# The causal convolution's spectra at 128 odd frequencies of 256 points, its wrapped end in one product, and two weight splits moved behind them

## The chip, the cores and the metric

The kernel runs on one core of a Trainium2 chip. The metric is the device time of one execution in microseconds. A core has an engine for matrix products (PE in the profile, its weight loads PEld), three engines for elementwise work (DVE, ACT, POOL) and SP, which here only issues transfers. The engines run their own instruction streams in order and wait for each other through semaphores.

## The reference

One decoder layer for 256 tokens of width 1024, all in float32: a norm, one input projection, then side by side an attention over 8 heads and a convolution module of 512 channels, an output projection with residual, and a SwiGLU network with residual. The part that matters here is the convolution and what surrounds it:

```
h = rms_norm(x, norm1_g)
proj = h @ w_in                        # q, k, v (512 each), u (1024)
a, g = split(u + glu_b)
h = a * sigmoid(g)                     # 256 tokens x 512 channels
h = causal_depthwise_conv(h, dw_w)     # 31 taps in the token direction
h = layer_norm(h + dw_b, ln_g, ln_b)   # over the 512 channels
conv = silu(h)
x = x + concat([attn, conv]) @ w_out
```

## The kernel before

Precision: the kernel writes most factors as a sum of a rounded high part and a low rest (names ending in `h` and `l`), and one product becomes three matmuls (`mm3`: high by high, high by low, low by high). Weights come from memory in blocks of 1 MB (`raw`), each of which is two pieces of 1024 columns. For a piece, ACT writes the high part `wh` and DVE the low part `wl`. `feed(n)` brings the pieces up to number `n` to their end; it is called ahead of the products, so that pieces are a few units ahead of PE. A block's buffer is free when the low part of its second piece has been written; then SP issues the load of the next block.

The order on every engine is that of the program text, and nothing reorders it later. Work beside the products is written as generator tasks; `step()` is called between groups of products and lets every task that is due write its next instructions.

The projections are five chunks of eight units (`p`, 40 units, pieces 0 to 19): k, q, the gate, the convolution's input, v. Tasks then compute the attention (`S`, `sm`, `p`, `pT`) while later chunks are still being multiplied. The output projection (`po`) uses pieces 20 to 27, and the network after it the rest.

The convolution is done with spectra. `spectra_task` turns the 31 taps into spectra `Ws` (one matmul, `pw`, for each of three column groups of the table `taps`). `conv_task` computes the gated input, splits it into `hh` and `hl`, and multiplies it by the table `fwd`: `hf` 0 and 1 are real and imaginary parts at 128 frequencies, `hf` 2 (in `third`, behind the v chunk) has the 17 frequencies that are left over from a transform of 288 points, 68 rows. DVE multiplies the spectra (`ya`, `yb`, `Y`), ACT and DVE split the products (`yh`, `yl`), and `ln_task` transforms back with the table `inv` into `cv` 0 and 1 (128 tokens each; three products of three matmuls for each), on which the channel norm stands (`st`, `mv`, `lr`, `nb`, `yn`). The bias `dw_b` is one row more in `Y` 2, against a row of ones in `inv`. `yn` is turned by PE into `cT`, in the middle of the first half of `po`.

Between `hf` 2 and `cv` PE computes the attention's output `O`: eight heads with two matmuls each in float32, with two heads in the two column halves of the array. `vs` is v scaled by ACT, in two halves for the two token blocks.

Of the kernel before, what the change touches and what calls it, by code (L numbers as in the profile page):

```python
# [9 lines left out]
F32R = mybir.dt.float32r  # L10
# [15 lines left out]
NF = FF // P  # L26
TAPS = 31
EPS = 1e-6
L = 288
NB = 47  # L30
BW = 2048
PIECE = 1024
R3 = 69
WARM = 18
RAW = 4
WGT = 7
# [14 lines left out]
GLU0_WAIT = 3  # L51
L1 = 8
L2 = 28
L3 = 34
W_FIRST = 1
SWAP = 31
SS_WAIT = 4
# [78 lines left out]
def _parts(a):  # L136

    hi = _round12(a)
    return np.stack([hi, a - hi], 1)


def _constants():
    t = np.arange(T)[:, None]
    f = np.arange(L // 2 + 1)[None, :]
    ang = 2 * np.pi * ((t * f) % L) / L
    c, s = np.cos(ang), np.sin(ang)
    alpha = np.where((f == 0) | (f == L // 2), 1.0, 2.0) / L
    fwd = np.concatenate([c[:, :P], -s[:, :P], c[:, P:], -s[:, P:], c[:, P:], -s[:, P:]], 1)
    fwd = _parts(fwd.astype(np.float32).reshape(NT, P, 324).transpose(1, 0, 2))
    ir, ii = (alpha * c).T, (-alpha * s).T  # L150
    inv = np.zeros((3, P, T))
    inv[0], inv[1] = ir[:P], ii[:P]
    inv[2, :R3] = np.concatenate([ir[P:], -ir[P:], ii[P:], ii[P:], np.ones((1, T))], 0)
    inv = _parts(inv.astype(np.float32).transpose(1, 0, 2))
    lag = (TAPS - 1 - np.arange(TAPS))[:, None]
    ang = 2 * np.pi * ((lag * f) % L) / L
    c, s = np.cos(ang), np.sin(ang)
    fw = np.concatenate([c[:, :P], -s[:, :P], c[:, P:], -s[:, P:], -s[:, P:], c[:, P:]], 1)
    fw = fw.astype(np.float32)
    hi = _round12(fw)  # L160
    taps = np.zeros((96, 324), np.float32)
    taps[0:TAPS], taps[32:32 + TAPS], taps[64:64 + TAPS] = hi, hi, fw - hi
    out = {"fwd": fwd, "inv": inv, "taps": taps}
    freq = np.power(np.float32(10000.0), -np.arange(0, HD, 2, dtype=np.float32) / np.float32(HD)).astype(np.float32)
    ang = np.arange(T, dtype=np.float32)[:, None] * freq[None, :]
    cos, sin = np.cos(ang.astype(np.float64)), np.sin(ang.astype(np.float64))
    tab = np.concatenate([cos, cos, -sin, sin], 1).astype(np.float32)
    out["rope"] = np.ascontiguousarray(tab.reshape(NT, P, 2 * HD).transpose(1, 0, 2))
    q, k = np.arange(P)[:, None], np.arange(P)[None, :]
    tri = np.where(k <= q, 0.0, -1e30)  # L170
    out["mask"] = np.concatenate([tri, np.zeros((P, P)), tri], 1).astype(np.float32)
    out["ident"] = np.eye(P, dtype=np.float32)
    return out
# [20 lines left out]
def _build(nc, tc, t, ctx):  # L194
# [12 lines left out]
    def t_bank(name, tag="t"):  # L207
        return psum.tile([P, 512], F32, name=name, tag=tag, bufs=2)
# [176 lines left out]
            load_next()  # L385
    ident = put(const, "ident", [P, P])
    load_next()
    taps = put(early, "taps", [96, 324], tag="Y", bufs=3)
    dwr = early.tile([96, W], F32, name="dwr", tag="Y", bufs=3)
    nc.sync.dma_start(dwr, t["dw_w"])  # L390
    mask = put(early, "mask", [P, 3 * P])
# [32 lines left out]
        G["cols"] = put(const, "cols", [P, 16])  # L424

    def spectra_task():
        tapr = early.tile([96, 324], F32R, name="tapr")
        nc.scalar.activation(tapr, taps, AF.Copy)
        dws = early.tile([96, W], F32R, name="dws")
        nc.scalar.activation(dws, dwr, AF.Copy)  # L430
        nc.vector.tensor_tensor(dws[32:64, :], dwr[32:64, :], dws[32:64, :].bitcast(F32), op=ALU.subtract)
        yield PW_GAP
        Ws = G["Ws"] = early.tile([P, 3, W], F32, name="Ws")
        for j, (o, n) in enumerate(spans):
            b = t_bank(f"pw{j}")
            nc.tensor.matmul(b[:n, :], tapr[:, o:o + n], dws, start=True, stop=True)
            nc.scalar.activation(Ws[:n, j, :], b[:n, :], AF.Copy)
            yield 1
# [50 lines left out]
    def q_task(banks):  # L489
        kqT = keep.tile([P, 2, 4, T], F32, name="kqT", tag="x2T")  # L490
        G["kT"], G["qT"] = kqT[:, 0], kqT[:, 1]
        qr, totals = [], []
        for i in range(NT):
            t1, total = rope_half(banks[i], 0, i, "q")
            totals.append(total)
            qr.append(t1)
            if i == 0:
                yield Q_GAP
        spawn(transposed(qr, G["qT"], "q"), QT_WAIT)
        yield 1  # L500
        for i in range(NT):
            r3 = heads3(G["kr"][i])
            nc.vector.tensor_tensor(r3, r3, cqk[1][:, i, :, None].to_broadcast([P, H, HD]), op=ALU.mult)
        spawn(transposed(G["kr"], G["kT"], "k"), KT_WAIT)
        yield 1
        for total in totals:
            total()
        mean_square(0)
        root(late_part)
        G["scq"] = early.tile([P, NT, H], F32, name="scq")  # L510
        nc.gpsimd.tensor_scalar(G["scq"], cqk[0], HD ** -0.5, None, op0=ALU.mult)
        for name, shape in (("fwd", [P, 2, NT, 324]), ("inv", [P, 2, 3, T])):
            tl = early.tile(shape, F32R, name=name)
            nc.gpsimd.dma_start(tl, t[name])
            G[name] = (tl[:, 0], tl[:, 1])
        yield S_WAIT
        G["sums"] = early.tile([P, NT, H], F32, name="sums")
        G["pT"] = [None] * H
        for j in range(H // 2):
            spawn(pair_task(j), 3 * j)  # L520
# [53 lines left out]
    def conv_task(banks):  # L574
# [3 lines left out]
        for i in range(NT):  # L578
# [6 lines left out]
                nc.vector.tensor_tensor(hl[:, 0, :], us[0], hh[:, 0, :].bitcast(F32), op=ALU.subtract)  # L585
            yield 1
        nc.vector.tensor_tensor(hl[:, 1, :], us[1], hh[:, 1, :].bitcast(F32), op=ALU.subtract)
        yield HF_WAIT
        fwd = G["fwd"]
        hf = []  # L590

        def spectrum(j):
            o, n = spans[j]
            b = t_bank(f"hf{j}", "s" if j < 2 else "t")
            for i in range(NT):
                mm3(b[:n, :], [f[:, i, o:o + n] for f in fwd], (hh[:, i, :], hl[:, i, :]), i == 0, i == NT - 1)
            hf.append(b)
# [12 lines left out]

        def third():

            spectrum(2)
            nc.vector.tensor_tensor(Y[2][:R3 - 1, :], hf[2][:R3 - 1, :], Ws[:R3 - 1, 2, :], op=ALU.mult)

        G["third"] = third
# [8 lines left out]

    def ln_task():
        inv = G["inv"]
        cv = []
        st = early.tile([P, NT, 6], F32, name="st")
        mv = early.tile([P, NT, 2], F32, name="mv")  # L630
        vv = early.tile([P, NT], F32, name="vv")
        for i in range(NT):
            b = t_bank(f"cv{i}", "s")
            for a, j in enumerate(range(3)):
                n = P if j < 2 else R3
                mm3(b, [m[:n, j, i * P:(i + 1) * P] for m in inv], G["ys"][j], a == 0, a == 2)
            cv.append(b)
        yield 1
        for i in range(NT):
            nc.vector.bn_stats(st[:, i, :], cv[i])  # L640
            nc.vector.bn_aggr(mv[:, i, :], st[:, i, :])
        nc.vector.tensor_scalar(vv, mv[:, :, 1], EPS, None, op0=ALU.add)
# [30 lines left out]
    for chunk in range(5):  # L673
        banks = [mm_bank(f"p{chunk}{i}") for i in range(NT)]
        for kt in range(KT):
            step()
            feed(unit // 2 + 1 if unit < L1 else (unit + 3) // 2 if unit < L2 else unit // 2 + (3 if unit < L3 else LEAD))
            w = wtile(unit * W, W)
            unit += 1
            sls = [slice(i * P, (i + 1) * P) for i in range(NT)]  # L680
            order = [(i, a) for i in range(NT) for a in range(3)]
            if W_FIRST < unit <= SWAP:
                order = [(0, 0), (0, 2), (1, 0), (1, 2), (0, 1), (1, 1)]
            for i, a in order:
                nc.tensor.matmul(banks[i], (xh, xh, xl)[a][:, kt, sls[i]], w[a % 2], start=kt == 0 and a == 0,  # L685
                                 stop=kt == KT - 1 and a == 2 - (order[-1][1] == 1))
        if after[chunk]:
            spawn(after[chunk](banks))
# [5 lines left out]
    G["third"]()  # L694
    mix = G["mix"] = [keep.tile([P, KT, T], F32R, name="mix" + s, tag="big_" + s) for s in "hl"]
    O = [None, None]
    for h in range(H):
        feed(unit // 2 + LEAD)
        if h % 2 == 0:
            step()  # L700
        base, pair = (h % 2) * HD, h // 2
        if h % 4 == 0:
            O[h // 4] = mm_bank(f"O{h // 4}").rearrange("p (a q) -> p a q", a=2)
        o = O[pair // 2][base:base + HD, pair % 2, :]
        hs = slice(h * HD, (h + 1) * HD)
        nc.tensor.matmul(o, vs[:, 0, hs], G["pT"][h][:, 0:T], start=True, stop=False)
        nc.tensor.matmul(o[:, P:], vs[:, 1, hs], G["pT"][h][:, T:], start=False, stop=True)
        if h % 4 == 3:
            sl = slice(pair - 1, pair + 1)
            split([m[:, sl, :] for m in mix], O[h // 4], nc.vector)  # L710
    spawn(ln_task())


# [243 lines left out]
def _layout(a):  # L957
# [26 lines left out]
    for n in ("q_norm_g", "k_norm_g"):  # L984
# [7 lines left out]
        "cols": np.concatenate([colize(A["norm2_g"][0]), colize(A["conv_ln_g"][0]), colize(A["conv_ln_b"][0])], 1),  # L992
        "glub": rep(A["glu_b"][0].reshape(2, W)),
        "gqk": rep(np.stack(gqk)),
        "dw_w": np.tile(np.concatenate([A["dw_w"][0], np.zeros((1, W), np.float32)], 0), (3, 1)),
        "dw_b": A["dw_b"],
    }

# [15 lines left out]
```

## Time and profile before

| | |
|---|---|
| runs | 290.14 us median of 3 (289.87 to 290.34) |
| profiled execution | 289.81 us, of which the span from first to last instruction is 288.0 us |
| granted PE clock | 1.00 |
| busy: PE, PEld, DVE, ACT, POOL | 282.5, 229.5, 225.9, 181.3, 24.9 us |
| DMA | 62.84 MB, 218 GB/s over the span |

PE's busy time counts matmuls whose ends are modelled, so 98% does not say that every matmul starts when it could. Start times tell more: consecutive matmuls with 512 columns start about 0.23 us apart, and a larger distance is a wait or a change of kind. In the rows of the timeline the first two columns are the start and the length in us; a number in brackets at a row's end is idle time of that engine before it and what ended it.

### The profile page before, as it was taken

The numbers are of one execution on the slowest core, as the hardware profiler recorded it, in microseconds if no ns is written. First come the engines' busy times: TensorE is split into PE (matmuls) and PEld (weight loads), VectorE is DVE, ScalarE is ACT, GpSimd is POOL, SyncE is SP. The second block draws the span as 40 slices with busy tenths as digits, with TensorE's granted clock in tenths as the row PEclk, the third lists the DMA queues.
The fourth block names the chain that finished last, engine by engine and source line by source line (L and its number), as shares of the span: only waits on it lengthen the run. The fifth ranks groups of instructions, "written<-read, shape, count | busy, mean of one in ns | idle before, by whom it ended". The sixth has DMA issues, their size and how long they took to land.

```text
span 288.0 us, 3690 instructions
## 1 busy us (share of the span) xinstructions
PE 282.5 (98%) x1321; PEld 229.5 (80%) x1321; DVE 225.9 (78%) x339; ACT 181.3 (63%) x271; POOL 24.9 (9%) x46
## 2 busy tenths in 40 slices
PE   8999999999999999999999999999999999999994
PEld 6878877778688888888888888888888888888883
DVE  3899995999973857999997868997787896887211
ACT  5777668989805778654987454795455496656000
POOL 0005473000000000011200011200001020000000
PEclk9999999999999999999999999999999999999999
DMA  7999968743804489368999746699864799400011
GB/s 243 415 413 361 366 218 300 259 152 109 333 1 146 152 316 390 104 216 166 227 352 412 294 150 109 185 229 403 303 259 140 131 239 332 151 1 2 0 73 74
DMA packets 12053, 62.84 MB, mean 218 GB/s; under 512 B 1602, under 2 KB 2210, under 8 KB 6275
## 3 DMA queue, kind: packets, MB, share of 16 engines
q1 hardware_dynamic: 9874, 54.86, 50.3%
q0 software_dynamic: 2016, 7.74, 14.1%
q8 instruction: 10, 0.16, 0.2%
q14 instruction: 9, 0.07, 0.1%
q10 hardware_dynamic: 144, 0.00, 0.0%
HBM read 61.55 MB, written 1.05 MB: 217 GB/s over the span
## 4 chain that ended last, share of the span: by engine, by line
PE 95%; DVE 3%; issue 1%
PE pd L724 21%; PE fg L724 19%; PE p L685 18%; PE U L724 11%; PE po L724 8%; PE V L724 6%; PE W L724 3%; PE aT L805 2%; PE warm L342 1%; PE S L528 1%; PE pT L558 1%; PE x2T L747 1%; PE cv L297 1%; DVE wl L278 0%; PE cv L298 0%
## 5 line engine op out<-in xcount | busy, mean ns | idle before, releaser
L273 ACT ACTIVATE wh<-raw 128x1024 fp32r<-128x1024 f32 x108 | 111.5, 1057 | 40.6 <-DVE raw L272 19.8
L278 DVE TENSOR_TENSOR wl<-raw,wh 128x1024 fp32r<-128x1024 f32 x108 | 129.3, 1221 | 9.3 <-ACT wh L273 8.7
L724 PE MATMUL pd<-wh,act 128*128 128x512 f32 x176 | 57.2, 393 | 0.0
L724 PE MATMUL fg<-wh,g 128*128 128x512 f32 x160 | 52.2, 393 | 0.0
L724 PEld LDWEIGHTS pd<-wh,act 128*128 128x128 f32 x176 | 33.0, 188 | 6.7
L724 PEld LDWEIGHTS fg<-wh,g 128*128 128x128 f32 x160 | 30.0, 188 | 6.1
L724 PE MATMUL pd<-wl,act 128*128 128x512 f32 x88 | 34.3, 389 | 0.0
L685 PE MATMUL p<-wh,xh 128*128 128x512 f32 x80 | 32.9, 412 | 0.0
L685 PE MATMUL p<-wh,xl 128*128 128x512 f32 x80 | 31.3, 392 | 0.0
L724 PE MATMUL fg<-wl,g 128*128 128x512 f32 x80 | 31.1, 389 | 0.0
L685 PE MATMUL p<-wl,xh 128*128 128x512 f32 x80 | 26.7, 395 | 0.0
L286 POOL DMA_DIRECT2D raw<-w x12 | 10.5, 879 | 177.7 <-DVE raw L272 153.3
L724 PEld LDWEIGHTS pd<-wl,act 128*128 128x128 f32 x88 | 16.5, 188 | 3.3
L685 PEld LDWEIGHTS p<-wh,xh 128*128 128x128 f32 x80 | 15.2, 189 | 3.5 <-issue 0.7
L810 DVE TENSOR_TENSOR act<-aT,act 128x512 fp32r<-128x512 f32 (+1 forms) x12 | 7.7, 646 | 12.9 <-ACT act L808 12.9
L685 PEld LDWEIGHTS p<-wl,xh 128*128 128x128 f32 x80 | 15.1, 189 | 3.2 <-DVE wl L278 0.3
L685 PEld LDWEIGHTS p<-wh,xl 128*128 128x128 f32 x80 | 15.1, 189 | 3.1
L724 PEld LDWEIGHTS fg<-wl,g 128*128 128x128 f32 x80 | 15.0, 188 | 3.0
L808 ACT ACTIVATE act<-aT 128x512 fp32r<-128x512 f32 (+1 forms) x12 | 6.6, 560 | 14.8 <-PE aT L805 14.8
L724 PE MATMUL U<-wh,g 128*128 128x512 f32 x48 | 15.8, 390 | 0.0
L272 DVE TENSOR_TENSOR raw<-raw,raw 128x1024 f32<-128x1024 f32 x12 | 14.6, 1218 | 0.0
L724 PE MATMUL po<-wh,mixh 128*128 128x512 f32 x32 | 12.6, 395 | 0.0
(179 smaller groups left out, 413.6 us busy)
## 6 DMA issues: line engine op xcount, KB each, us to landing
raw<-w SPq DMA_DIRECT2D x45, 1024.0 KB, 5.3
raw<-w POOLq DMA_DIRECT2D x12, 512.0 KB, 5.5
first<-first SPq DMA_DIRECT2D x8, 384.0 KB, 6.1
xtok<-xtok SPq DMA_DIRECT2D x2, 512.0 KB, 9.1
x<-xtok SPq DMA_DIRECT2D x2, 512.0 KB, 6.0
out<-o SPq DMA_DIRECT2D x4, 256.0 KB, 2.0
inv<-inv POOLq DMA_DIRECT2D x1, 768.0 KB, 6.9
fwd<-fwd POOLq DMA_DIRECT2D x1, 648.0 KB, 4.0
```

Source lines behind the costliest of these rows:

```text
L272: nc.vector.tensor_tensor(src, src, blocks[add][:, cut(a)], op=ALU.add)
L273: nc.scalar.activation(dst[0], src, AF.Copy)
L278: nc.vector.tensor_tensor(dst[1], src, dst[0].bitcast(F32), op=ALU.subtract)
L286: nc.gpsimd.dma_start(blocks[to][:, cut(a)], t["w"][more - 2][:, cut(a)], accum_op=ALU.add)
L297: nc.tensor.matmul(out, lhs[0], rhs[1], start=False, stop=False)
L342: nc.tensor.matmul(warm[:, 0:T], zeros[:, 0:P], zeros, start=True, stop=True)
L528: nc.tensor.matmul(banks[a][:, out], G["qT"][rows, j, q], G["kT"][rows, j, k], start=True, stop=True)
L685: nc.tensor.matmul(banks[i], (xh, xh, xl)[a][:, kt, sls[i]], w[a % 2], start=kt == 0 and a == 0, stop=kt == KT - 1 and a == 2 - (order[-1] ...
L724: nc.tensor.matmul(bank, l, r, start=start and a == 0, stop=stop and a == 2, skip_group_check=on)
L805: nc.tensor.transpose(b[:, a, :], u[:, a * P:(a + 1) * P], ident)
L808: nc.scalar.activation(hi, b[:, 0:nf, :], AF.Copy)
L810: nc.vector.tensor_tensor(lo, b[:, 0:nf, :], hi.bitcast(F32), op=ALU.subtract)
```

## The change

The transform goes from 288 points to 256 points at the odd multiples of half a step, of which 128 are enough. A product of such spectra is a convolution that wraps with a changed sign: the first 30 outputs get the last taps' share of the last 30 inputs, subtracted. This wrapped end is taken out by a second, small transform of 60 points: the last 32 token rows of `hh`, `hh` and `hl` are copied by three transfers of the POOL queue into three groups of 32 partitions of a new tile `tail`, and `hf` 2 is one matmul of 96 rows against a table `ends` with 120 columns, high and low parts together. Since only the first 30 tokens need it, `cv` 1 (tokens 128 to 255) has no product with `Y` 2; its bias comes from one matmul of the taps' tile `dws` (whose spare rows now hold `dw_b`) with 128 columns more in `tapr`. `cv` 1 is computed ahead of `cv` 0. `Ws`, `Y` and `yl` of index 2 have 120 or 121 rows for 68 or 69; `taps` and `tapr` have 504 columns for 324; `fwd` has 256 columns for 324.

Two things are moved besides. `feed` no longer runs one piece further from unit 34 on, and isn't called between the heads of `O`, so that pieces 23 and 24 get their low parts behind the spectra, and pieces 24 and 25 their high parts. The matmuls of `O` are written with the two heads of a pair in turn.

The core of the diff:

```diff
-L = 288
-R3 = 69
+WRAP = 60
+R3 = 2 * WRAP + 1
+COLS = 2 * P + 2 * WRAP
...
-L3 = 34
...
+    c, s = odd(T, np.arange(T))
+    fwd = _parts(np.concatenate([c, -s], 1).astype(np.float32).reshape(NT, P, T).transpose(1, 0, 2))
...
-    taps = put(early, "taps", [96, 324], tag="Y", bufs=3)
+    taps = put(early, "taps", [96, COLS + P], tag="Y", bufs=3)
...
-        for name, shape in (("fwd", [P, 2, NT, 324]), ("inv", [P, 2, 3, T])):
+        for name, shape in (("fwd", [P, 2, NT, T]), ("ends", [96, R3 - 1]), ("inv", [P, 2, 3, T])):
...
+        tail = early.tile([96, W], F32R, name="tail")
+        for a, part in enumerate((hh, hh, hl)):
+            nc.gpsimd.dma_start(tail[32 * a:32 * a + 32, :], part[96:, 1, :])
         yield HF_WAIT
...
-            spectrum(2)
+            b = t_bank("hf2")
+            hf.append(b)
+            nc.tensor.matmul(b[:R3 - 1, :], G["ends"], tail, start=True, stop=True)
...
-        for i in range(NT):
-            b = t_bank(f"cv{i}", "s")
-            for a, j in enumerate(range(3)):
-                n = P if j < 2 else R3
-                mm3(b, [m[:n, j, i * P:(i + 1) * P] for m in inv], G["ys"][j], a == 0, a == 2)
-            cv.append(b)
+        cv = [t_bank(f"cv{i}", "s") for i in range(NT)]
+        for j in range(2):
+            mm3(cv[1], [m[:, j, P:] for m in inv], G["ys"][j], j == 0, False)
+        nc.tensor.matmul(cv[1], G["tapr"][:, COLS:], G["dws"], start=False, stop=True)
+        for j in range(3):
+            mm3(cv[0], [m[:P if j < 2 else R3, j, :P] for m in inv], G["ys"][j], j == 0, j == 2)
         yield 1
-        for i in range(NT):
+        for i in (1, 0):
             nc.vector.bn_stats(st[:, i, :], cv[i])
...
-            feed(unit // 2 + 1 if unit < L1 else (unit + 3) // 2 if unit < L2 else unit // 2 + (3 if unit < L3 else LEAD))
+            feed(unit // 2 + 1 if unit < L1 else (unit + 3) // 2 if unit < L2 else unit // 2 + 3)
...
-    for h in range(H):
-        feed(unit // 2 + LEAD)
-        if h % 2 == 0:
-            step()
...
+    for pair in range(H // 2):
+        step()
...
+        for i in range(NT):
+            for odd in range(2):
+                h = 2 * pair + odd
+                o = O[pair // 2][odd * HD:(odd + 1) * HD, pair % 2, i * P:]
+                nc.tensor.matmul(o, vs[:, i, h * HD:(h + 1) * HD], G["pT"][h][:, i * T:i * T + T - i * P],
+                                 start=i == 0, stop=i == 1)
```

Where rows move. On DVE, before, between the multiplied spectra and the statistics of the channel norm:

```order
L614 TENSOR_TENSOR Y2_869<-hf2_896,Ws_509 68x512
L278 TENSOR_TENSOR wl24_856<-raw12_616,wh24_855 128x1024
L255 TENSOR_TENSOR yl_911<-Y0_867,yh_910 128x512
L255 TENSOR_TENSOR yl_911<-Y1_868,yh_910 128x512
L255 TENSOR_TENSOR yl_911<-Y2_869,yh_910 69x512
L255 TENSOR_TENSOR mixl_905<-O0_918,mixh_904 128x512
L255 TENSOR_TENSOR mixl_905<-O1_929,mixh_904 128x512
L640 BN_STATS st_944<-cv0_947 128x6
```

The same place of DVE after the change (the names are the same; `wl23` stood ahead of the first `ya` before):

```order
L624 TENSOR_TENSOR Y2_869<-hf2_896,Ws_511 120x512
L260 TENSOR_TENSOR yl_902<-Y0_867,yh_901 128x512
L260 TENSOR_TENSOR yl_902<-Y1_868,yh_901 128x512
L260 TENSOR_TENSOR yl_902<-Y2_869,yh_901 121x512
L260 TENSOR_TENSOR mixl_900<-O0_909,mixh_899 128x512
L260 TENSOR_TENSOR mixl_900<-O1_920,mixh_899 128x512
L283 TENSOR_TENSOR wl23_858<-raw11_583,wh23_857 128x1024
L283 TENSOR_TENSOR wl24_957<-raw12_618,wh24_956 128x1024
L649 BN_STATS st_935<-cv1_939 128x6
```

Two low parts of weights have moved from ahead of `yl` to behind `mixl`, and the statistics stand behind them.

On ACT, before, from the scaled v to the channel norm:

```order
L692 ACTIVATE vs_893<-p40_694,c_179 128x512
L693 ACTIVATE vs_893<-p41_695,c_179 128x512
L273 ACTIVATE wh25_906<-raw12_616 128x1024
L254 ACTIVATE yh_910<-Y0_867 128x512
L254 ACTIVATE yh_910<-Y1_868 128x512
L254 ACTIVATE yh_910<-Y2_869 69x512
L254 ACTIVATE mixh_904<-O0_918 128x512
L254 ACTIVATE mixh_904<-O1_929 128x512
L273 ACTIVATE wh26_1002<-raw13_715 128x1024
L650 ACTIVATE yn0_1020<-cv0_947,nb_992,lr_980 128x512
```

And after:

```order
L701 ACTIVATE vs_893<-p40_696,c_179 128x512
L702 ACTIVATE vs_893<-p41_697,c_179 128x512
L259 ACTIVATE yh_901<-Y0_867 128x512
L259 ACTIVATE yh_901<-Y1_868 128x512
L259 ACTIVATE yh_901<-Y2_869 121x512
L259 ACTIVATE mixh_899<-O0_909 128x512
L259 ACTIVATE mixh_899<-O1_920 128x512
L278 ACTIVATE wh24_956<-raw12_618 128x1024
L278 ACTIVATE wh25_959<-raw12_618 128x1024
L278 ACTIVATE wh26_1001<-raw13_717 128x1024
L659 ACTIVATE yn0_1019<-cv0_938,nb_991,lr_979 128x512
```

The high part of piece 25 has gone from ahead of `yh` to behind `mixh`, and that of piece 24, which stood further up, has joined it. On SP one load of a weight block (`raw16`) goes from ahead of the transfers of `dw_b` and of the residual's tokens to behind them, since it waits for `wl23`.

More of the change, by code (lines that the diff above doesn't have):

```diff
@@ L142, in _constants @@
 def _constants():
[L143 to L150, printed above, removed]
-    inv = np.zeros((3, P, T))
-    inv[0], inv[1] = ir[:P], ii[:P]
@@ L153, in _constants, with odd @@
-    inv[2, :R3] = np.concatenate([ir[P:], -ir[P:], ii[P:], ii[P:], np.ones((1, T))], 0)
-    inv = _parts(inv.astype(np.float32).transpose(1, 0, 2))
[L155 to L159, printed above, removed]
+    def odd(n, at):
+        ang = np.pi * ((np.arange(n // 2)[None, :] * 2 + 1) * np.asarray(at)[:, None] % (2 * n)) / n
+        return np.cos(ang), np.sin(ang)
@@ new lines, in _constants @@
+    c, s = odd(T, np.arange(T))
+    fwd = _parts(np.concatenate([c, -s], 1).astype(np.float32).reshape(NT, P, T).transpose(1, 0, 2))
+    inv = np.zeros((3, P, T))
+    inv[0], inv[1] = 2 / T * c.T, -2 / T * s.T
+    wrapped = np.arange(TAPS - 1)
+    c, s = (2 / WRAP * a.T for a in odd(WRAP, TAPS - 1 + wrapped))
+    inv[2, :R3 - 1, :TAPS - 1] = np.concatenate([c, -c, -s, -s], 0)
+    inv[2, R3 - 1, :P] = 1
+    inv = _parts(inv.astype(np.float32).transpose(1, 0, 2))
+    c, s = odd(WRAP, wrapped)
@@ L160, in _constants @@
+    ends = np.zeros((32, R3 - 1), np.float32)
+    ends[32 - len(wrapped):] = np.concatenate([c, -s, c, -s], 1)
+    hi = _round12(ends)
+    ends = np.concatenate([hi, ends - hi, hi], 0)
+    lag = TAPS - 1 - np.arange(TAPS)
+    (c, s), (cw, sw) = odd(T, lag), odd(WRAP, lag)
+    fw = np.concatenate([c, -s, cw, -sw, -sw, cw], 1).astype(np.float32)
     hi = _round12(fw)
-    taps = np.zeros((96, 324), np.float32)
-    taps[0:TAPS], taps[32:32 + TAPS], taps[64:64 + TAPS] = hi, hi, fw - hi
-    out = {"fwd": fwd, "inv": inv, "taps": taps}
+    taps = np.zeros((96, COLS + P), np.float32)
@@ L164, in _constants @@
+    taps[0:TAPS, :COLS], taps[32:32 + TAPS, :COLS], taps[64:64 + TAPS, :COLS] = hi, hi, fw - hi
+    taps[TAPS, COLS:] = taps[32 + TAPS, COLS:] = 1
+    out = {"fwd": fwd, "inv": inv, "ends": ends, "taps": taps}
     freq = np.power(np.float32(10000.0), -np.arange(0, HD, 2, dtype=np.float32) / np.float32(HD)).astype(np.float32)
@@ L426, in spectra_task @@
     def spectra_task():
-        tapr = early.tile([96, 324], F32R, name="tapr")
+        tapr = G["tapr"] = early.tile([96, COLS + P], F32R, name="tapr")
         nc.scalar.activation(tapr, taps, AF.Copy)
-        dws = early.tile([96, W], F32R, name="dws")
+        dws = G["dws"] = early.tile([96, W], F32R, name="dws")
         nc.scalar.activation(dws, dwr, AF.Copy)
@@ L511, in q_task @@
         nc.gpsimd.tensor_scalar(G["scq"], cqk[0], HD ** -0.5, None, op0=ALU.mult)
-        for name, shape in (("fwd", [P, 2, NT, 324]), ("inv", [P, 2, 3, T])):
+        for name, shape in (("fwd", [P, 2, NT, T]), ("ends", [96, R3 - 1]), ("inv", [P, 2, 3, T])):
             tl = early.tile(shape, F32R, name=name)
             nc.gpsimd.dma_start(tl, t[name])
-            G[name] = (tl[:, 0], tl[:, 1])
+            G[name] = tl if name == "ends" else (tl[:, 0], tl[:, 1])
         yield S_WAIT
@@ L593, in spectrum @@
             o, n = spans[j]
-            b = t_bank(f"hf{j}", "s" if j < 2 else "t")
+            b = t_bank(f"hf{j}", "s")
             for i in range(NT):
@@ L627, in ln_task @@
         inv = G["inv"]
-        cv = []
         st = early.tile([P, NT, 6], F32, name="st")
@@ L696, in _build @@
     O = [None, None]
-    for h in range(H):
-        feed(unit // 2 + LEAD)
-        if h % 2 == 0:
-            step()
[L701 to L708, printed above, removed]
+    for pair in range(H // 2):
+        step()
+        if pair % 2 == 0:
+            O[pair // 2] = mm_bank(f"O{pair // 2}").rearrange("p (a q) -> p a q", a=2)
+        for i in range(NT):
[4 more added lines that the diff above has]
+                                 start=i == 0, stop=i == 1)
+        if pair % 2:
             sl = slice(pair - 1, pair + 1)
-            split([m[:, sl, :] for m in mix], O[h // 4], nc.vector)
+            split([m[:, sl, :] for m in mix], O[pair // 2], nc.vector)
     spawn(ln_task())
@@ L994, in _layout @@
         "gqk": rep(np.stack(gqk)),
-        "dw_w": np.tile(np.concatenate([A["dw_w"][0], np.zeros((1, W), np.float32)], 0), (3, 1)),
+        "dw_w": np.tile(np.concatenate([A["dw_w"][0], A["dw_b"]], 0), (3, 1)),
         "dw_b": A["dw_b"],
```

## The prediction

> **What bounds the kernel now.** I read the page first, then the chain of work that ended last, then the timeline where that chain leaves PE.
>
> ```profile
> PE 282.5 (98%) x1321; PEld 229.5 (80%) x1321; DVE 225.9 (78%) x339; ACT 181.3 (63%) x271; POOL 24.9 (9%) x46
> PE 95%; DVE 3%; issue 1%
> ```
>
> PE carries 95% of the chain. So a matmul taken from PE is worth its distance to the next one, unless PE then waits for something else. The chain shows one place, the one that is changed, where it runs through DVE (start, length, what):
>
> ```profile
> 70.60 0.55 DVE p L554 x2
> 71.15 1.13 DVE wl L278
> 72.28 0.60 DVE ya L607
> ...
> 77.79 0.69 DVE yl L255
> 78.53 0.50 PE cv L297
> ...
> 82.75 8.18 PE po L724 x36
> 90.93 0.87 PE cT L661 x8
> ```
>
> From 70.60 to 78.53 DVE decides: attention weights, a low part of weights, the multiplied spectra, then `yl`, for which the second matmul of `cv` waits. After 82.75 the chain is PE to the end. So what counts is when `po` starts. PE there:
>
> ```profile
> 73.52 0.39 PE L296 MATMUL hf<-hh,fwd 128*68 128x512 f32 x1
> 74.67 0.40 PE L298 MATMUL hf<-hh,fwd 128*68 128x512 f32 x1
> 74.99 0.66 PE L706 MATMUL O<-pTs,vs 128*64 128x256 f32 x4
> 75.47 0.39 PE L707 MATMUL O<-pTs,vs 128*64 128x128 f32 x4
> 77.80 0.50 PE L296 MATMUL cv<-yh,inv 128*128 128x512 f32 x1
> 78.53 0.50 PE L297 MATMUL cv<-yl,inv 128*128 128x512 f32 x1 [0.23 <-DVE yl L255]
> 78.86 0.39 PE L298 MATMUL cv<-yh,inv 128*128 128x512 f32 x1
> 82.59 0.40 PE L724 MATMUL po<-wh,mixh 128*128 128x512 f32 x1
> ```
>
> The six matmuls of `hf` 2 start 1.15 us apart from first to last (0.23 each), `O` takes 2.81 from its first matmul to `cv`, and the first two of `cv` stand 0.73 apart where 0.23 is normal: that is the wait for `yl`.
>
> **The change, part by part.** *hf 2, six matmuls to one.* `O` can follow the one as it followed the sixth, 0.32 behind: 73.52 + 0.32 = 73.84 instead of 74.99, so 1.15 less. The price of a matmul goes by its 512 columns: 68, 120 or 128 columns of weights make no difference that the rows above show (0.39 either way).
>
> *What O waits for then.* ACT's rows:
>
> ```profile
> 69.70 1.05 ACT L273 ACTIVATE wh<-raw 128x1024 fp32r<-128x1024 f32 x1
> 73.02 0.69 ACT L692 ACTIVATE vs<-p,c 128x512 f32<-128x512 f32 x1 [0.20 <-PE p L685]
> 73.72 0.69 ACT L693 ACTIVATE vs<-p,c 128x512 f32<-128x512 f32 x1
> 77.06 0.63 ACT L254 ACTIVATE yh<-Y 69x512 fp32r<-69x512 f32 x1 [0.26 <-DMA Y<-dw_b]
> 86.10 1.45 ACT L650 ACTIVATE yn<-cv,nb,lr 128x512 f32<-128x512 f32 x2 [6.49 <-DVE nb L645]
> ```
>
> The first half of `vs` is done at 73.71, in time; the second at 74.41. Both wait for PE's last projections, so neither comes earlier. The matmuls of the second half follow the first by 0.48 (74.99 to 75.47), which would be 74.32; with 0.05 for the signal they start at 74.46: 0.14 lost. Five matmuls fewer had covered that. `cv` then starts at 77.80 - 1.15 + 0.14 = 76.79.
>
> *The new order of O's matmuls.* I cost it at nothing, because the rows show four matmuls of L706 ahead of the first of L707, though the program had L707 of a head ahead of L706 of the next: the pair of heads already goes side by side. Were there a gain, `yl` below would hold it up.
>
> *Low parts moved on DVE.* DVE's rows from the last low part ahead of the spectra:
>
> ```profile
> 71.07 1.22 DVE L278 TENSOR_TENSOR wl<-raw,wh 128x1024 fp32r<-128x1024 f32 x1
> 72.20 0.68 DVE L607 TENSOR_TENSOR ya<-hf,Ws 128x512 f32<-128x512 f32 x1
> 76.66 1.21 DVE L278 TENSOR_TENSOR wl<-raw,wh 128x1024 fp32r<-128x1024 f32 x1
> 77.79 1.89 DVE L255 TENSOR_TENSOR yl<-Y,yh 128x512 fp32r<-128x512 f32 x3
> 79.60 1.28 DVE L255 TENSOR_TENSOR mixl<-O,mixh 128x512 fp32r<-128x512 f32 x2
> 82.79 0.70 DVE L640 BATCH_NORM_STATS2 st<-cv 128x6 f32<-128x512 f32 x1 [1.09 <-PE cv L298]
> ```
>
> Two low parts leave this stretch, but only one of them is a full gain. Ahead of `ya` the last low part is now that of piece 22, and its high part takes the place on ACT of the one at 69.70, behind the exponentials, which wait for DVE as before. So it is ready at 70.75, DVE starts at 70.78, and `ya` follows 1.13 later (71.07 to 72.20): 71.91 instead of 72.20, 0.29 earlier. From `ya` to the end of the last `Y`'s slot are 4.46 (72.20 to 76.66), and no low part stands there any more: `yl` at 76.37, done with 0.68 at 77.05. Its high part `yh` is no obstacle: ACT reaches it behind `vs`, at 74.4.
>
> *The start of cv.* The second matmul would come at 76.79 + 0.33 = 77.12 by itself (the first distance behind another kind of matmul is 0.32 to 0.33 in the rows above), and at 77.10 by `yl`. So PE waits no longer, but the two are level. Before, 0.73 + 0.33 lay from the first to the third; now 0.33 + 0.23, which is 0.50 less.
>
> *cv, 18 matmuls to 16.* From 78.86 to 82.59 are 16 distances, 0.233 each; two fewer are 0.47.
>
> *Sum.* -1.15 + 0.14 - 0.50 - 0.47 = -1.98, `po` at 80.61. Against the profiled 289.81 that is 287.83; the runs' median lies 0.33 above that execution, so 288.2 for the runs.
>
> *The tail copies.* They are new on the path: `hf` 2 can't start before all three have landed, and `O`, `cv` and all behind stand in PE's queue.
>
> ```profile
> 62.88 0.64 ACT L582 ACTIVATE hh<-ua 128x512 fp32r<-128x512 f32 x1 [0.16 <-DVE ua L581]
> 64.09 0.69 DVE L587 TENSOR_TENSOR hl<-ua,hh 128x512 fp32r<-128x512 f32 x1
> 44.41 0.77 POOL L514 DMA_DIRECT2D fwd<-fwd  x1
> 45.17 0.57 POOL L514 DMA_DIRECT2D inv<-inv  x1
> inv<-inv POOLq DMA_DIRECT2D x1, 768.0 KB, 6.9
> fwd<-fwd POOLq DMA_DIRECT2D x1, 648.0 KB, 4.0
> dwr<-dw_w SPq DMA_DIRECT2D x1, 192.0 KB, 12.3
> ```
>
> `hh` is done at 63.52, `hl` at 64.78. POOL has nothing else queued then; at up to 0.77 an issue the third goes out at about 65.1, 8.4 us ahead of the need at 73.5. No copy within the core's own memory is in this trace; the nearest rows are the two POOL transfers, 4.0 and 6.9 us for ten times the bytes, and the longest of any is 12.3. I take 4 to 6.9, landing at 69 to 72, and cost it at nothing; the lower bound is nothing too, the upper 65.1 + 12.3 - 73.5 = 3.9 us.
>
> ```profile
> 41.73 1.19 POOL L310 TENSOR_TENSOR c<-c,ca 128x16 f32<-128x16 f32 x1
> 42.99 0.22 POOL L307 TENSOR_TENSOR ca<-c 128x16 f32<-128x16 f32 x1
> 41.62 1.21 DVE L278 TENSOR_TENSOR wl<-raw,wh 128x1024 fp32r<-128x1024 f32 x1
> ```
>
> POOL's issue could be slower than that: the same tiny operation takes 1.19 beside DVE's `wl` and 0.22 without it. Were each issue to cost that 0.97 more, the third would begin at 67.0 and land 7.9 later at 74.9: 1.4 us lost. Against it, `inv` was issued in 0.57. The Trainium skill has a rule that speaks against the copies here ("DMA: Bandwidth & Descriptors", section on SWDGE vs HWDGE vs iDMA): POOL writes the descriptors of its transfers into that memory itself, and DVE's two-port operations lock it out meanwhile. By it the sum would be -1.98 as long as the lockouts stay under the 8.4 us of lead, and the row agrees that there is such a lock, without showing it on an issue.
>
> *Covered edits.* `tapr` has 180 columns more on ACT:
>
> ```profile
> 34.55 0.47 ACT L428 ACTIVATE tapr<-c_taps 96x324 fp32r<-96x324 f32 x1
> 38.90 0.60 ACT L480 ACTIVATE kqT<-kT 128x512 f32<-128x512 f32 x1 [1.23 <-PE kT L479]
> ```
>
> At 0.47 for 324 that is at most 0.26, inside the 1.23 that ACT idles before 38.90. Without that cover the transposed k would be later, and `S` with it. `Ws` and `Y` 2 have more rows and the same 512 columns, so the same time. `fwd` is smaller, `ends` one issue more on POOL 20 us early. On SP `raw16` goes out when `wl23` is done, at about 80.6, where it went out around 72.3 before; `dw_b` and the tokens pass it and come earlier. What stands behind it on SP, the next block, waits for `wl25` until 87 anyway. Landing in some 5 to 7 us it is there by 88, and its first piece, 30, is ten pieces behind the start of `po`, at 12 matmuls of 0.227 each 27 us later. Piece 23 is needed three pieces in, 80.6 + 8.2 = 88.8, and its low part is done at 80.6.
>
> *What is late next.* The statistics stand behind two low parts. DVE ends `mixl` at about 79.4 (1.4 earlier than before: yl0 is 1.42 earlier), the low parts take 2.3 to 81.7, the two statistics and their small sums reach 83.4; before, 82.79 + 0.70 = 83.49. So `yn` ends at 87.5 as before, while `cT` moves from 90.93 to 88.95: 3.4 us of slack become 1.5.
>
> **Rivals.** *DVE stays the bound.* For it: the two times at `cv` are 0.02 apart. If DVE gains only the low part between `Y` and `yl`, `yl` is done 0.29 later and so is `po`: 288.5. If it gains nothing, only the two matmuls of `cv` are saved: 289.7. I hold the first possible, the second not, since the row of 76.66 goes in any case.
>
> *The copies come late.* Every microsecond behind 73.5 is one lost, and from a landing at 75.5 on the kernel is slower; at the 12.3 us of the longest row it is 290.1 - 2.0 + 3.9 = 292.0. Against it: that row queued with megabytes on SP's queue, and POOL's is empty.
>
> *The norm comes late.* If the statistics don't hide the low parts at all, `yn` is 2.3 later than counted and eats the 1.5: 0.8 of loss, 289.0. Against it: DVE idled 1.09 before the second statistics and is 1.4 early.
>
> **How the numbers follow.** My forecast has 0.70, DVE as the bound 0.14, the copies late 0.07, the norm late 0.07, other causes 0.02. A difference under 0.2% (0.58 us) can't be told from none. The runs spread by 0.25 to either side; with that the forecast alone reaches from 287.7 to 288.6. Towards DVE's case and the norm's the range goes to 289.1; below, `yl` at 77.10 forbids much more, so 287.5. Faster holds the forecast, nearly all of DVE's and the norm's cases and a small lateness of the copies, 0.88; within 0.2%, 0.06; slower, the late copies for the most part, 0.06.
>
> **What would show it.** One matmul of `hf` 2 at 73.5 and no idle time before it; `O` 0.3 behind, with a short wait for `vs`; `cv` at about 76.8 with its second matmul about 0.33 behind; 16 of them; `po` at 80.6; `yn` at 86.0 and PE without a gap before `cT`. Wrong if PE waits for `tail` or at `cT`, or if the second matmul of `cv` still waits for `yl` by more than 0.1.

## The result: 2.6 us faster, and the profile after

The changed kernel takes 287.61 us in the median of 4 runs (287.36 to 287.81) against 290.24 us; the ratio is 0.9909, with a 95% interval of 0.9892 to 0.9926. A second measurement gave 287.58 us against 289.90, 0.9915 (0.9900 to 0.9931). The profiled execution has 287.53 us with a span of 285.7, 2.3 less than before. Two executions on record, 476.46 us of the kernel before and 404.57 of the run with twelve copies below, had a mean granted clock of 0.56 and 0.66; they are in the medians of their runs and in no ratio.

The page, engines and chain of work that ended last, after the change:

```profile
PE 280.8 (98%) x1314; PEld 228.1 (80%) x1314; DVE 226.0 (79%) x339; ACT 181.6 (64%) x271; POOL 26.9 (9%) x50
PE 98%; DVE 0%; issue 0%
```

The 3% of the chain that ran through DVE are gone: PE carries all of it. The place of the change in PE's timeline (start, length, what; idle time before it would stand in brackets):

```profile
73.32 0.40 PE L694 MATMUL p<-wh,xl 128*128 128x512 f32 x1
73.56 0.40 PE L623 MATMUL hf<-tail,ends 96*120 96x512 f32 x1
73.89 3.00 PE L714 MATMUL O<-pTs,vs 128*64 128x256 f32 x32
76.81 0.50 PE L301 MATMUL cv<-yh,inv 128*128 128x512 f32 x1
77.16 0.39 PE L302 MATMUL cv<-yl,inv 128*128 128x512 f32 x1
77.39 0.39 PE L303 MATMUL cv<-yh,inv 128*128 128x512 f32 x1
80.66 0.39 PE L732 MATMUL po<-wh,mixh 128*128 128x512 f32 x1
```

From the last matmul of the projections to the first of `po` are 7.34 us; 9.31 before. The second matmul of `cv` follows the first by 0.35 and waits for nothing. DVE and ACT there:

```profile
70.68 1.23 DVE L283 TENSOR_TENSOR wl<-raw,wh 128x1024 fp32r<-128x1024 f32 x1 [0.65 <-ACT wh L278]
71.82 0.68 DVE L615 TENSOR_TENSOR ya<-hf,Ws 128x512 f32<-128x512 f32 x1
76.27 1.89 DVE L260 TENSOR_TENSOR yl<-Y,yh 128x512 fp32r<-128x512 f32 x3
79.27 2.35 DVE L283 TENSOR_TENSOR wl<-raw,wh 128x1024 fp32r<-128x1024 f32 x2
85.65 1.45 ACT L659 ACTIVATE yn<-cv,nb,lr 128x512 f32<-128x512 f32 x2 [4.82 <-DVE nb L654]
```

`yl` has moved from 77.79 to 76.27, and the two low parts stand behind it at 79.27. The end of the span moved further than the work. DVE's last output, before:

```profile
283.97 0.69 DVE L953 TENSOR_TENSOR o<-pd,x 128x512 f32<-128x512 f32 x1 [2.03 <-PE pd L724]
```

and after:

```profile
282.02 0.69 DVE L961 TENSOR_TENSOR o<-pd,x 128x512 f32<-128x512 f32 x1 [2.03 <-PE pd L732]
```

It is 1.95 us earlier, the span's end 2.3: from the end of this row to that of the span were 3.37 us and are 3.00. The difference lies between two signals of POOL in the closing handshake of the engines (single records of the traces), 0.42 apart before and 0.08 after.

### The profile page after: what moved, and what is told of

Its sections match the earlier page's. It is cut to its first block, busy times and chain, and to the rows that moved or that the text cites. A ratio compares the mean times of both kernels' runs of the same rounds, so it can differ in the third digit from the quotient of the medians.

```text
span 285.7 us, 3692 instructions
## 1 busy us (share of the span) xinstructions
PE 280.8 (98%) x1314; PEld 228.1 (80%) x1314; DVE 226.0 (79%) x339; ACT 181.6 (64%) x271; POOL 26.9 (9%) x50
## 4 chain that ended last, share of the span: by engine, by line
PE 98%; DVE 0%; issue 0%
PE pd L732 21%; PE p L694 20%; PE fg L732 19%; PE U L732 11%; PE po L732 8%; PE V L732 6%; PE W L732 3%; PE aT L813 2%; PE warm L347 1%; PE S L533 1%; PE pT L563 1%; PE O L714 1%; PE x2T L755 1%; PE cv L301 0%; PE cv L303 0%; PE cv L302 0%
## 5 line engine op out<-in xcount | busy, mean ns | idle before, releaser
L818 DVE TENSOR_TENSOR act<-aT,act 128x512 fp32r<-128x512 f32 (+1 forms) x12 | 7.7, 644 | 12.9 <-ACT act L816 12.9
```

Source lines behind the costliest of these rows:

```text
L818: nc.vector.tensor_tensor(lo, b[:, 0:nf, :], hi.bitcast(F32), op=ALU.subtract)
```

## The experiments

Executions differ by up to 0.9 us in when the last projection matmul starts (73.1 to 74.0). Most of that is there by the 31st of the 240 projection matmuls (12.1 to 12.9), long before anything that an experiment here changes; its cause was not looked into. So the traces are compared by the distance from the last projection matmul to the first of `po` (below: the distance), which is 9.31 before, from this row of PE's timeline to the one at 82.59,

```profile
73.28 0.40 PE L685 MATMUL p<-wh,xl 128*128 128x512 f32 x1
```

and 7.34 after.

**Each part alone.** The theory: `po` starts by the later of PE's own queue and `yl`. First the moved pieces alone, in the kernel before:

```diff
-feed(... unit // 2 + (3 if unit < L3 else LEAD))
+feed(... unit // 2 + 3)
...
     for h in range(H):
-        feed(unit // 2 + LEAD)
```

> The kernel before with one part of the change, the low parts of weights behind the spectra (and their high parts behind mixh). Theory (po starts when the later of two is there: PE's own queue, or yl for the second matmul of cv): yl is done 1.5 us earlier, at 76.95, but PE reaches the second matmul of cv only at 78.13, so only the wait of 0.50 goes: po at 82.1, 0.5 us faster than before, 289.7. Rival (only PE's count of matmuls matters): 290.2, as before. Rival (the chain through DVE alone sets the end): 288.7.

Measured: 289.83 us, ratio 0.9989 (0.9978 to 1.0001), distance 8.83, so 0.48 saved. PE's timeline:

```profile
73.75 0.40 PE L685 MATMUL p<-wh,xl 128*128 128x512 f32 x1
...
78.26 0.51 PE L296 MATMUL cv<-yh,inv 128*128 128x512 f32 x1
78.61 0.39 PE L297 MATMUL cv<-yl,inv 128*128 128x512 f32 x1
78.83 0.40 PE L298 MATMUL cv<-yh,inv 128*128 128x512 f32 x1
...
82.58 0.39 PE L723 MATMUL po<-wh,mixh 128*128 128x512 f32 x1
```

The wait for `yl` at the start of `cv` is gone (from the first matmul to the third 0.57 us for 1.06) and nothing else. The interval of the time reaches just over 1, so it is the trace that shows it. Then all of the change but the moved pieces:

```diff
-feed(... unit // 2 + 3)
+feed(... unit // 2 + (3 if unit < 34 else LEAD))
...
     for pair in range(H // 2):
+        feed(unit // 2 + LEAD)
         step()
```

> The changed kernel with the pieces ahead of the spectra again, as before. Theory: PE has seven matmuls fewer, but yl is done at 78.47 as before, so PE waits for it at the second matmul of cv for about 1.4 us; only the two matmuls of cv behind that wait are saved, and po starts at 82.1: 289.7, 0.5 us faster than before, 2.1 slower than the changed kernel. So either part alone is worth 0.5 and both together 2.0 or more. Rival (PE's count of matmuls): seven matmuls fewer, 288.6.

Measured: 289.30 us, ratio 0.9975 (0.9964 to 0.9986), distance 8.81, so 0.50 saved. The time also holds the 0.37 at the end of the span, which comes with the three transfers (below). PE and DVE:

```profile
73.75 0.40 PE L694 MATMUL p<-wh,xl 128*128 128x512 f32 x1
...
77.25 0.50 PE L301 MATMUL cv<-yh,inv 128*128 128x512 f32 x1
78.96 0.51 PE L302 MATMUL cv<-yl,inv 128*128 128x512 f32 x1 [1.22 <-DVE yl L260]
...
82.56 0.39 PE L733 MATMUL po<-wh,mixh 128*128 128x512 f32 x1
```

```profile
77.09 1.22 DVE L283 TENSOR_TENSOR wl<-raw,wh 128x1024 fp32r<-128x1024 f32 x1
78.22 1.89 DVE L260 TENSOR_TENSOR yl<-Y,yh 128x512 fp32r<-128x512 f32 x3
```

PE has its seven matmuls fewer and reaches `cv` early, only to wait 1.7 us from its first matmul to its second, because a low part stands ahead of `yl`. The parts give 0.48 and 0.50 alone and 1.97 together: more than twice their sum. The rival that only PE's count matters (1.6 us for this part) and the rival that only DVE's chain matters (1.5 for the other) both fall.

**PE has no slack left.** Two of the saved groups of matmuls put back, in the changed kernel, without touching DVE:

```diff
-            nc.tensor.matmul(b[:R3 - 1, :], G["ends"], tail, start=True, stop=True)
+            for _ in range(6):
+                nc.tensor.matmul(b[:R3 - 1, :], G["ends"], tail, start=True, stop=True)
```

> The changed kernel with the one matmul of hf 2 issued six times over, same result. Theory: O starts 1.15 us later, no longer waits for vs (0.12), cv's second matmul at 78.2, yl long there: po 1.0 us later, 288.6. Rival (DVE's chain is the bound and PE has slack there): no change, 287.6.

Measured: 288.70 us, ratio 0.9956 (0.9940 to 0.9973), distance 8.30: 0.96 later.

```diff
+        for _ in range(2):
+            nc.tensor.matmul(cv[1], inv[1][:R3, 2, P:], G["ys"][2][0], start=False, stop=False)
         nc.tensor.matmul(cv[1], G["tapr"][:, COLS:], G["dws"], start=False, stop=True)
```

> The changed kernel with two matmuls more in cv 1, with zeros from the table inv, so that cv has 18 as before. Theory: po 0.47 us later, 288.1; yn later by nothing, since the statistics of cv 1 wait for DVE's low parts anyway. Rival (slack): 287.6.

Measured: 288.12 us, ratio 0.9936 (0.9921 to 0.9950), distance 7.80: 0.46 later. Both as the theory has it; five matmuls cost 0.96 and not 1.15, since with them `O` doesn't wait for `vs` (2.75 us from its first matmul to `cv`, for 2.92).

**The order of O's matmuls.** Head after head again:

```diff
-        for i in range(NT):
-            for odd in range(2):
+        for odd in range(2):
+            for i in range(NT):
```

> The changed kernel with O's matmuls in the order of before, head after head. Theory (the two heads of a pair go side by side in either order, as the trace of before shows): O takes as long, 287.6, and at most 0.1 slower or faster by where the wait for the second half of vs falls. Rival (matmuls of one column half in a row can't go beside those of the other, so order counts): O up to 1.3 us longer, 288.9.

Measured: 288.15 us, ratio 0.9939 (0.9926 to 0.9951), distance 7.76: 0.42 later. Neither expectation was right.

```profile
73.52 0.40 PE L694 MATMUL p<-wh,xl 128*128 128x512 f32 x1
74.08 3.43 PE L714 MATMUL O<-pTs,vs 128*64 128x256 f32 x32
77.44 0.50 PE L301 MATMUL cv<-yh,inv 128*128 128x512 f32 x1
```

`O` to `cv` is 3.36 us for 2.92. The view by stretches, of `O`'s records alone, counts what ran ahead of the second half of `vs` (a stretch and its length, then PE's busy time and records, the granted PE clock, the DMA share and GB/s), with head after head and then in the changed kernel:

```profile
74.08:74.68 0.60, 0.60 (x2) 1.00 1.09 437
```

```profile
73.88:74.48 0.60, 0.59 (x4) 1.00 1.07 430
```

Each of these matmuls leaves two records, so one head got through its first block in the one case and both did in the other. The single records say the same. In the changed kernel the two heads of a pair start together throughout (73.885 and 73.892, 74.152 and 74.158, then the second half of `vs`: 74.495 and 74.502). With head after head, the first head starts at 74.080 and 74.347, its second block waits until 74.690 for the second half of `vs`, which ACT finishes at 74.638, and the other head, whose first block needed nothing of that half, starts only at 74.697, behind it. From there the second column half runs one block late, to the end, where its last head runs alone (the first half's last record starts at 76.800, the second's last three at 76.914 to 77.239). In the kernel before, nothing was waited for, and the halves ran side by side in the same order (74.992 and 75.005). Without a wait the old order takes 2.81 us there, and 2.80 in the run with the moved pieces alone; the new order takes 2.75 with `hf` 2 issued six times. So order alone is worth some 0.06, and the rest hangs on the wait; no run has the old order without the wait in the changed kernel itself. That the two halves overlap in either order is right; that the order is therefore free is wrong as soon as a matmul waits.

**How much lead the tail copies have.** Twelve or thirty small copies on POOL ahead of them:

```diff
+        scr = early.tile([P, 100], F32, name="scr")
+        for _ in range(12):    # and 30
+            nc.gpsimd.tensor_scalar(scr, us[1][:, 0:100], 1.0, None, op0=ALU.mult)
         for a, part in enumerate((hh, hh, hl)):
             nc.gpsimd.dma_start(tail[32 * a:32 * a + 32, :], part[96:, 1, :])
```

In the changed kernel itself the transfers land 2 us after issue (the trace's list of transfers: KB each, us to landing), the last by 67.0:

```profile
tail<-hh POOLq DMA_DIRECT2D x2, 64.0 KB, 2.0
tail<-hl POOLq DMA_DIRECT2D x1, 64.0 KB, 1.9
```

> The changed kernel with twelve small copies of 100 columns on POOL ahead of the three transfers into tail, which makes them later by some 4 us. Theory: the transfers landed at 67.0 and are needed at 73.5, so 6.5 us of lead: no change, 287.6. Rival (they are close to the path): slower by what they come later, 291.

> The same with thirty copies, later by some 10 us. Theory: beyond the lead of 6.5 us every microsecond counts: hf 2 starts when the last transfer has landed, O, cv and po behind it; a landing at 77 gives 291.1, and the time is 287.6 plus landing minus 73.5. Rival (other work is put in between, or the norm hides it): less than half of that.

Measured: 295.17 us (1.0162, 1.0137 to 1.0188) and 302.74 us (1.0446, 1.0430 to 1.0462). The delays were larger than planned, 9.3 and 19.4 us instead of 4 and 10, since a small copy on POOL took 0.7 to 0.8 us. So the first run doesn't test the lead from inside: its last transfer landed at 77.9. In its profiled execution (293.55 us; two others took 1.5 and 1.7 longer, at a mean granted clock of 0.987 for 0.992) PE stood:

```profile
78.06 0.46 PE L626 MATMUL hf<-tail,ends 96*120 96x512 f32 x1 [4.03 <-DMA tail<-hl]
78.45 4.50 PE L717 MATMUL O<-pTs,vs 128*64 128x256 f32 x32
82.88 0.50 PE L301 MATMUL cv<-yh,inv 128*128 128x512 f32 x1
86.71 0.39 PE L735 MATMUL po<-wh,mixh 128*128 128x512 f32 x1
```

`hf` 2 is 4.5 us late, `po` 6.05 and the execution 6.0. The other 1.5 are in `O`, which takes 4.43 to `cv` for 2.92. The view by stretches shows why (a stretch and its length, then the busy time of PE, PEld, DVE, ACT and POOL, then the granted PE clock, the DMA share and GB/s). With twelve copies:

```profile
74.00:78.00 4.00, 0.03 (x1) 0.00 (x0) 2.06 (x4) 0.90 (x3) 0.59 (x2) 1.00 0.81 299
78.06:79.12 1.06, 1.06 (x9) 0.67 (x11) 0.56 (x1) 0.94 (x2) 0.00 (x0) 1.00 0.05 15
79.14:82.54 3.40, 3.40 (x24) 2.34 (x22) 2.60 (x5) 1.23 (x2) 0.00 (x0) 0.50 0.00 0
82.56:84.00 1.44, 1.44 (x11) 1.09 (x8) 0.37 (x1) 1.00 (x2) 0.00 (x0) 1.00 0.00 0
```

With thirty:

```profile
74.00:78.00 4.00, 0.00 (x0) 0.00 (x0) 1.90 (x4) 0.61 (x1) 3.42 (x8) 1.00 0.59 239
78.00:82.00 4.00, 0.00 (x0) 0.00 (x0) 0.00 (x0) 0.00 (x0) 3.42 (x8) 0.50 0.00 0
86.27:91.68 5.41, 5.41 (x29) 3.44 (x31) 3.19 (x5) 1.85 (x4) 0.00 (x0) 0.50 0.01 3
91.70:94.00 2.30, 2.30 (x15) 1.78 (x12) 1.24 (x2) 1.87 (x3) 0.00 (x0) 1.00 0.00 0
```

In both runs PE's clock is granted at half after PE has idled for about 4 us. With twelve copies PE idles for 4.0 us, works for 1.1 at the full clock and then for 3.4 at half; the records of `O` with 256 columns start 0.43 us apart there, for 0.22 at the full clock. With thirty the clock falls 4.2 us into the idling and stays at half for the first 5.4 us of work. With thirty copies `hf` 2 is 12.7 late and `po` 15.2. So the copies do stand in the path once the lead is used up, and a long wait costs more than its length. The rival (less than half) falls, and so does the expectation of one for one.

**The norm.** Additions of 512 columns ahead of its statistics on DVE, whose results nothing uses:

```diff
+        scr = work("scr", "tmp", 6)
+        for _ in range(4):
+            nc.vector.tensor_tensor(scr, wtile(21 * PIECE, W)[0].bitcast(F32), wtile(21 * PIECE, W)[1].bitcast(F32), op=ALU.add)
         for i in (1, 0):
             nc.vector.bn_stats(st[:, i, :], cv[i])
```

> The changed kernel with four additions of 512 columns on DVE (2.4 us) ahead of the channel norm's statistics. Theory: yn was done 1.7 us ahead of cT, so cT is 0.7 us late and the kernel 0.7 slower, 288.3. Rival (the norm has more room than that, since PE can do other products): 287.6. Rival (the norm is close to the path): 2.4 slower, 290.0.

Measured: 288.87 us, ratio 0.9962 (0.9949 to 0.9976), 1.3 us slower than the changed kernel beside it. PE now waits twice at `cT`, where it waited for nothing (`cT` at 88.82 in the changed kernel, 1.72 us behind the end of `yn` at 87.10):

```profile
89.11 0.33 PE L673 MATMUL cT<-c_ident,yn 128*128 128x128 f32 x1 [0.28 <-ACT yn L662]
89.78 0.98 PE L673 MATMUL cT<-c_ident,yn 128*128 128x128 f32 x7 [0.34 <-ACT yn L662]
```

The additions took 2.86 us in place of 2.4 and made `yn` 2.8 later, so with 1.7 of slack 1.1 were to be lost; from the last projection matmul to DVE's last output it is 1.1 more (210.5 for 209.4). The slack is as read.

**The closing handshake.** Tiny memsets on POOL in the kernel before, three and then one:

```diff
+        pad = early.tile([P, 1], F32, name="pad")
+        for _ in range(3):    # and 1
+            nc.gpsimd.memset(pad, 0.0)
         yield HF_WAIT
```

> The kernel before with three tiny memsets of 128x1 on POOL at the place where the change has its three transfers; nothing else differs. The changed kernel gained 0.34 us between the end of its last transfer and the end of the span: POOL's last handshake took 0.42 before and 0.08 after. Theory (POOL's instructions lie differently in memory when there are more of them, and the last ones need not be fetched any more): the handshake shrinks to 0.08 and the kernel is 0.3 faster, 289.9. Rival (that was chance, or has another cause): 0.42 again, 290.2.

> The kernel before with one tiny memset of 128x1 on POOL instead of three. Theory (any instruction more on POOL moves the last ones to another place): the last handshake of POOL takes 0.08 here too. Rival (it takes as many more as the three): 0.42. The time of one run is not read.

Measured: 289.80 us with three, ratio 0.9994 (0.9983 to 1.0004), too little to tell by time. DVE's last output with three and with one, in spans of 288.13 and 287.54:

```profile
284.44 0.69 DVE L956 TENSOR_TENSOR o<-pd,x 128x512 f32<-128x512 f32 x1 [2.03 <-PE pd L727]
```

```profile
283.84 0.69 DVE L956 TENSOR_TENSOR o<-pd,x 128x512 f32<-128x512 f32 x1 [2.03 <-PE pd L727]
```

From its end to the span's are 3.00 and 3.01, and 2.99 to 3.01 in every profile of a kernel with the three transfers; it is 3.37 in the kernel before and 3.38 in that with the moved pieces alone, where POOL's program has its old length. So one instruction more on POOL takes 0.37 us off the end, and three take off no more. Why isn't shown; that the last instructions then lie elsewhere in memory is a guess that no row here tests.

**The changed kernel again, and a small step further.**

> The changed kernel once more, beside the kernel before on the same chip. po starts 7.34 us behind the last projection matmul (9.31 before), which is 1.97, and POOL's last handshake gives 0.37: 2.3 us in all, a ratio of 0.992. Rival (the 2.6 us between the first medians are all the kernel's): 0.991.

Measured: 287.58 us, ratio 0.9915 (0.9900 to 0.9931), distance 7.33, and 2.99 us from DVE's last output to the end of the span. Both ratios hold the 2.34 us that the traces show (0.9919).

The wait of `O` for the second half of `vs` can be filled with `cv` 1's bias matmul:

```diff
             nc.tensor.matmul(b[:R3 - 1, :], G["ends"], tail, start=True, stop=True)
+            G["cv1"] = t_bank("cv1")
+            nc.tensor.matmul(G["cv1"], G["tapr"][:, COLS:], G["dws"], start=True, stop=False)
...
-        cv = [t_bank(f"cv{i}", "s") for i in range(NT)]
+        cv = [t_bank("cv0", "s"), G["cv1"]]
...
-        nc.tensor.matmul(cv[1], G["tapr"][:, COLS:], G["dws"], start=False, stop=True)
```

> The changed kernel with the bias matmul of cv 1 moved ahead of O, right behind hf 2, in a bank of another tag. Theory: it fills the 0.12 us in which O waits for the second half of vs, so po starts 0.12 earlier and the time is 287.5, less than a measurement tells; the trace shows 7.22 from the last projection matmul to po for 7.34. Rival (the first switch to O's kind of matmul costs more that way): 7.34 or more.

Measured: 287.44 us, ratio 0.9921 (0.9906 to 0.9935): no difference that the times can tell. The trace has a distance of 7.15 (73.34 to 80.49), 0.19 less where 0.12 was expected, and `O` without a wait, 2.75 us to `cv`:

```profile
73.81 0.40 PE L625 MATMUL cv<-dws,tapr 96*128 96x512 f32 x1
74.13 2.82 PE L715 MATMUL O<-pTs,vs 128*64 128x256 f32 x32
76.88 0.50 PE L301 MATMUL cv<-yh,inv 128*128 128x512 f32 x1
```

## Why the prediction was right, and where not

- *What bounds the kernel.* PE, except where DVE held `yl`: shown by the two parts alone, which give 0.48 and 0.50, and together 1.97.
- *The sum.* -1.98 forecast up to `po`, -1.97 measured by the distance. Term by term, measured and in brackets forecast: from `hf` 2 to `O` -1.14 (-1.15); from `O` to `cv` +0.11 (+0.14); from the first matmul of `cv` to the third -0.48 (-0.50); from there to `po` -0.46 (-0.47). The wait for `vs` itself is 0.12, from 74.158 to 74.495 where 0.216 is the normal distance, and `yl` was done at 76.95 (77.05).
- *The new order of O at nothing: this step failed.* It is worth 0.42 us behind a wait. I read rightly that the pair of heads goes side by side before, and concluded that order is free; but the same part had just made `O` wait for `vs`, and a waiting matmul holds back the other column half behind it. That the sum came out in this term is luck: the 0.14 takes for granted that both heads' first blocks run ahead of the waiting second block, and with the wait only the new order does that. With the old order the distance falls by 1.55 and not by 1.97. Nor did `yl` hold the 0.42 up, as I thought it would: it was done at 76.95, 0.2 ahead of `cv`'s second matmul at 77.16.
- *The forecast of the time was 0.6 too high* (288.2 for 287.6, just inside the range of 287.5 to 289.1). The term missing from the sum is the end of the span, 0.37. Nearly all of the rest is the 0.33 that I added for the median of the runs over the profiled execution; here it was 0.08, a difference within what runs differ by.
- *Tail copies at nothing:* right; they land at 67.0, where 69 to 72 was taken from transfers ten times their size. Their issue took 0.49 to 0.51 us each beside a busy DVE and 0.50 to 0.54 in the run with thirty copies, where DVE idled, so nothing held it up. By the rule of the Trainium skill ("DMA: Bandwidth & Descriptors", SWDGE vs HWDGE vs iDMA) two-port operations of DVE would have. No row shows whether DVE ran one then, and the row of 1.19 that I read as agreeing shows a POOL operation beside `wl`, not the writing of descriptors. The price that I put on lateness, one for one, was too low: after 4.0 us of idle PE the clock fell as well.
- *What is late next:* the norm, with 1.5 us forecast and 1.7 measured (`yn` done at 87.10 for 87.5, `cT` at 88.82 for 88.95), and the added work lost what the slack didn't hold.

## What to carry to other kernels

Where two queues meet at one instruction, price each part of a change with the other undone: here each half was worth a quarter of the whole by the traces, and the time of the first alone couldn't be told from no change. When work is taken from ahead of a wait, look again at everything that the work had covered, the order of the instructions behind it among it. Give a new transfer in the path a lead that is several microseconds, since a wait that slows PE's clock, as 4.0 us of it did here, costs more than its length.

## What the runs showed of the hardware

Matmuls in the two column halves overlap in the order of before as well, and they then don't start in the order of the program text: the second head's first block starts at 75.005, ahead of the first head's second at 75.475. But a matmul that waits holds up later ones of the other half, and the halves then stay one block apart to the end of the group: 0.42 us here.

PE's granted clock went to half 4.2 us into the idling in one run, and in the other after 4.0 us of idling and 1.1 of work. It came back 3.4 us after it had fallen in the second, and 5.4 us after work had begun again in the first. The Trainium skill ("TensorE: Matmul & The Clock Gate", Part 1: The HAM clock gate) gives half the clock after at least one idle window of about 3.4 us, and the full clock after at least one busy window of that length. None of the times here is shorter than that; why they differ from each other no run here tests.

A transfer of 64 KB within the core's own memory through POOL's queue took 1.9 us with hardly anything beside it (41 GB/s with its own bytes, in the run with thirty copies), 1.9 to 2.1 where transfers ran at 406 GB/s for 1.2 us after the first issue (the changed kernel), and 3.8 to 4.5 where they ran at 403 GB/s for 3.4 us after it (twelve copies). And 0.37 us at the end of a span hung on one instruction more on POOL.
